# A decoder step on one core: head in a written-out order, norm sums by one ones product, padded mixing, attention projections with features on partitions

## The chip, the core and the metric

One core of a Trainium2 chip runs the whole step as one program. Its engines are TensorE (PE in the profile, PEld for its weight loads), VectorE (DVE), ScalarE (ACT), GpSimd (POOL) and SyncE (SP), which issues the transfers. The metric is the device time of one execution in microseconds; lower is better.

## The reference, cut to what matters

There are 256 prompt tokens and 64 sample tokens (320 in all, `NT`), a model width of 2048, and two layers. Everything is float32.

```python
# layer 0: gMLP over chunks of 128 tokens            # layer 1: sparse attention
z = gelu(rmsnorm(x) @ w_in);  u, v = halves(z)       p = rmsnorm(x) @ w_in;  q,k,v,iq,ik,iw = split(p)
v = rmsnorm(v)                                        q = rope(rmsnorm_per_head(q)); k = the same; iq, ik = rope
s = tril(w_s[g]) @ v_g + b_s   (per group g)          score = sum_h relu(iq_h . ik) * iw_h ; keep the top 64 (66)
x += (u * s) @ w_out                                  x += softmax(q k / sqrt(128), kept keys only) v @ w_o
# after each layer: x += (silu(conv3(g)) * conv3(up)) @ w_out,   g, up = halves(rmsnorm(x) @ w_in)
```

Outputs are x, the new keys, values and indexer keys of layer 1, the normalised v rows of layer 0 and the last rows before each convolution. `rmsnorm` divides by the root of the mean square over the features; `rope` turns each head's first half against its second half by angles that depend on the token.

## The kernel before, in words

Activations lie with features on the 128 partitions and the 320 tokens along the free axis: `xT` is 16 such tiles. Each weight block of 128x128 is the stationary operand of a matmul over 320 columns. For the precision of float32 every operand is split in two parts of the matmul's reduced type: weights in `wh` (a copy by ACT) and `wl` (the rest, by DVE), activations in `hh` and `hl` (or `rh` and `rl`). Each block then takes three matmuls, `wh·hh`, `wh·hl`, `wl·hh`, which the profile names `mm`. There are 17,328 of them. All other matmuls (`sd` in the profile: transposes, sums over partitions by a product with ones, attention scores) go to two PSUM banks of their own, `mm` results to six.

Weights arrive in units of 1 MB. A unit is split in two half-units, and 24 `mm` belong to each. `split(n + 2)` is written two half-units ahead of the matmuls that use it, and `wh` and `wl` have three buffers, so the ACT copy for half-unit n+3 can start when the matmuls of half-unit n are done. The 512 output columns of four units are one group of four PSUM banks.

Everything else is written as Python generators (`b_tile`, `norm_fin` and so on) that a small planner class (`Side`) resumes at every second block of `mm`; `yield PE` says that the next step begins with a matmul. The planner keeps an estimate of each engine's load and decides at which place in the instruction order a step is put. `S.ensure(flag)` resumes all tasks at once until the flag is there: it is called where an `mm` needs a free bank (`("ev", nbank - 6)`), or an input that a task makes (`(("o", gi), j)`: the attention of head group gi). The order that results is fixed in the program; engines run their own queues in that order.

The places that the change touches:

- The head: `x_load`, `x_tile` and the first loop passes. Tile f of x is scaled by the gain into `hh` and `hl`, squared on ACT and added into `acc` by POOL. `norm_fin(0)` then makes the factor `rs` that every result of the first stage is multiplied with when it leaves its bank.
- `norm_fin`, four times: sums over partitions by three products with a ones column, a Newton chain on 128x3 numbers, three diagonal matrices `dg`, three products with ones that spread the factors over partitions, one copy into `rs`.
- `u_tile`, 16 times: the mixing `s`. Two products of 128 rows and one of 64 rows (the sample tokens).
- Layer 1: groups in the order iq0, ik, iq1, k, v, q0, q1, q2, then the output projection o0, then q3, o1, o2, o3. For iq, k, q and v, four result tiles (heads) are collected in `tB`; `to_tok` transposes them to tokens on partitions (three bursts of four transposes), DVE applies norm and rope there, and `to_feat` transposes back (three bursts more, not for v). q and k heads also take three products with ones each for the norm.
- `attn_prompt` and `attn_sample`: four and two tasks per head group; o0 needs all six of head group 0.

Of the kernel before, what the change touches and what calls it, by code (L numbers as in the profile page):

```python
# [174 lines left out]
def trunk(ctx: ExitStack, tc: tile.TileContext, i, o):  # L175
# [60 lines left out]
    dg = com(3, 128)  # L236
# [68 lines left out]
    def norm_fin(st):  # L305
        r = tok_rstd(acc, D)
        for tt in range(3):
            w = TOKW[tt]
            dve.tensor_scalar(dg[0:w, tt, 0:w], ident[0:w, 0:w], r[0:w, tt:tt + 1], None, op0=ALU.mult)
        yield PE  # L310
        ps = sd()
        for tt in range(3):
            w = TOKW[tt]
            pe.matmul(ps[:, tt * 128:tt * 128 + w], lhsT=ones[0:w, :], rhs=dg[0:w, tt, 0:w], start=True, stop=True)
        dve.tensor_copy(rs, ps[:, 0:NT])
        S.set(("rs", st))
# [63 lines left out]
    def x_load(f, n):  # L380
        sp.dma_start(xT[:, f:f + n], i["xT"][:, f:f + n])
        for k in range(f, f + n):
            x_time[k] = S.load["dma"] + 2.2

    x_time = {}

    def x_tile(f):
        g = gT[:, f:f + 1]
        if f > 3:
            S.cur.t = x_time[f]  # L390
            yield 1
# [3 lines left out]
        yield 1  # L395
        q = yield from square_acc(("n", 0), xT[:, f], acc)
        yield 1
        add_acc(acc, q, pool)
        cnt["h", 0] = cnt.get(("h", 0), 0) + 1
        if cnt["h", 0] == NK:  # L400
            S.add(norm_fin(0), 2)

    def ws_prep():
        yield from wait(("rs", 0))
        sp.dma_start(wsT, i["a_w_sT"])
# [54 lines left out]
    def u_tile(f, ps):  # L460
# [12 lines left out]
        pe.matmul(p2[:, 256:320], lhsT=v_tok[0:64, 2, f * 128:(f + 1) * 128], rhs=wsS[0:64, f, :], start=True, stop=True)  # L473
# [161 lines left out]
    rC = cB(3, 128)  # L635
    rS = cB(3, 128)
    yn = [cB(512) for _ in range(2)]
    t2 = cB(512)
    tB = [cB(NT) for _ in range(4)]
    ssq = [cB(4, 3) for _ in range(2)]  # L640
    rq = cB(4, 3)
    rqt = cB(12)
    gq = cB(128)
# [11 lines left out]
    CM, CMS, SelH, Tm, Rep, BM = (cst[:, 0:256], cst[0:64, 256:520], cst[0:16, 520:648], cst[:, 648:712],  # L655
                                  cst[0:64, 712:968], cst[0:64, 968:1032])
    r64C, r64S = cI(3, 64), cI(3, 64)
# [3 lines left out]
    iwT = cI(64)  # L661
# [20 lines left out]
    def fold(g):  # L682
        sp.dma_start(rC, i["c_rope"][:, :, 0:128])
        sp.dma_start(rS, i["c_rope"][:, :, 128:256])
        sp.dma_start(gq, g.partition_broadcast(128))
        yield 1
        dve.tensor_tensor(rC, rC, gq[:, None, :].to_broadcast([128, 3, 128]), op=ALU.mult)
        for a, b in ((0, 64), (64, 0)):
            dve.tensor_tensor(rS[:, :, a:a + 64], rS[:, :, a:a + 64], gq[:, None, b:b + 64].to_broadcast([128, 3, 64]),
                              op=ALU.mult)  # L690

    def b_prep():
        sp.dma_start(pt_sb[0:1, :].bitcast(I32), i["page_table"])
        sp.dma_start(cst, i["c_idx"])
        sp.dma_start(r64C, i["c_rope"][:, :, 256:320])
        sp.dma_start(r64S, i["c_rope"][:, :, 320:384])
        for s in ssq:
            dve.memset(s, 1.0)
# [5 lines left out]
        yield from fold(i["b_k_norm"][0])  # L704
        S.set("gk")

    def rope(src, y, p, n, half, C, Sn):

        d = 2 * half
        sv = src.rearrange("p (h d) -> p h d", d=d)  # L710
        yv = y[0:p, 0:n * d].rearrange("p (h d) -> p h d", d=d)
        tv = t2[0:p, 0:n * d].rearrange("p (h d) -> p h d", d=d)
        dve.tensor_tensor(tv[:, :, 0:half], sv[:, :, half:d], Sn[:, None, 0:half].to_broadcast([p, n, half]), op=ALU.mult)
        dve.tensor_tensor(tv[:, :, half:d], sv[:, :, 0:half], Sn[:, None, half:d].to_broadcast([p, n, half]), op=ALU.mult)
        dve.tensor_tensor(yv, sv, C[:, None, :].to_broadcast([p, n, d]), op=ALU.mult)
        dve.tensor_tensor(yv, yv, tv, op=ALU.add)

    def to_tok(tt):
        w = TOKW[tt]
        ps = sd()  # L720
        for c in range(4):
            pe.transpose(ps[0:w, c * 128:(c + 1) * 128], tB[c][:, tt * 128:tt * 128 + w], ident)
        return ps

    def to_feat(y, tt):
        w = TOKW[tt]
        ps = sd()
        for c in range(4):
            pe.transpose(ps[:, c * 128:c * 128 + w], y[0:w, c * 128:(c + 1) * 128], ident[0:w, 0:w])
        return ps  # L730

    def b_tile(kind, gi, c, ps):
        yield from wait(("rs", 2))
        if c == 0:
            yield from take("tB")
        else:
            yield from wait(("tB", kind, gi))
        S.set(("tB", kind, gi))
        dve.tensor_tensor(tB[c], ps[:, 0:NT], rs, op=ALU.mult)
        evd(ps)  # L740
        if kind in "qk":
            yield 1
            b = yield from take("sq", 2)
            q = sqr[b]
            act.activation(q, tB[c], AF.Square)
            yield PE
            p2 = sd()
            for tt in range(3):
                w = TOKW[tt]
                pe.matmul(p2[0:w, tt:tt + 1], lhsT=q[:, tt * 128:tt * 128 + w], rhs=ones[:, 0:1], start=True, stop=True)  # L750
            s = ssq[gi % 2]
            dve.tensor_copy(s[:, c, 0:2], p2[:, 0:2])
            dve.tensor_copy(s[0:64, c, 2:3], p2[0:64, 2:3])
            give("sq", b)
        cnt["tB", kind, gi] = cnt.get(("tB", kind, gi), 0) + 1
        if cnt["tB", kind, gi] == 4:
            S.add({"iq": iq_group, "k": qk_group, "q": qk_group, "v": v_group}[kind](gi), 1)

    def iq_group(gi):
        yield from wait("bprep")  # L760
        yield from take("tok")
        for tt in range(3):
            w = TOKW[tt]
            y = yn[tt % 2]
            ps = to_tok(tt)
            if tt == 2:
                give("tB", 0)
            rope(ps[0:w, :], y, w, 8, 32, r64C[0:w, tt], r64S[0:w, tt])
            yield PE
            p2 = to_feat(y, tt)  # L770
            pv = p2.rearrange("p (c t) -> p c t", t=128)
            if tt < 2:
                copy_act(iqT(gi)[:, :, tt * 128:tt * 128 + 128], pv)
            else:
                copy_act(iqS()[:, :, 32 * gi:32 * gi + 32].rearrange("p b (c t) -> p c b t", t=8),
                         pv[:, :, 0:64].rearrange("p c (b t) -> p c b t", t=8))
            yield 1
        give("tok", 0)
# [6 lines left out]
    def v_group(gi):  # L785
        yield from take("tok")
        for tt in range(3):
            w = TOKW[tt]
            ps = to_tok(tt)
            if tt == 2:  # L790
                give("tB", 0)
            copy_act(V[0:w, tt], ps[0:w, :])
            yield 1
            sp.dma_start(o["new_v_sample"] if tt == 2 else o["new_v_prompt"][tt * 128:(tt + 1) * 128], V[0:w, tt])
        give("tok", 0)
        S.set("v")

    def qk_group(gi):
        isk = gi < 0
        yield from wait("gk" if isk else "gq")  # L800
        if gi > 1:
            yield from wait((("o", gi - 2), 0))
        yield from take("tok")
        v = ssq[gi % 2].rearrange("p a b -> p (a b)")
        dve.tensor_scalar(v, v, 1.0 / 128, EPS, op0=ALU.mult, op1=ALU.add)
        r = rq.rearrange("p a b -> p (a b)")
        rsqrt(v, r, rqt)
        yield PE
        for tt in range(3):
            w = TOKW[tt]  # L810
            y = yn[tt % 2]
            ps = to_tok(tt)
            if tt == 2:
                give("tB", 0)
            pv = ps[0:w, :].rearrange("p (h d) -> p h d", d=128)
            dve.tensor_tensor(y[0:w].rearrange("p (h d) -> p h d", d=128), pv, rq[0:w, :, tt:tt + 1].to_broadcast([w, 4, 128]),
                              op=ALU.mult)
            yield 1
            rope(y[0:w], y, w, 4, 64, rC[0:w, tt], rS[0:w, tt])
            if isk:  # L820
                sp.dma_start(o["new_k_sample"] if tt == 2 else o["new_k_prompt"][tt * 128:(tt + 1) * 128], y[0:w])
            yield PE
            p2 = to_feat(y, tt)
            pv = p2.rearrange("p (c t) -> p c t", t=128)
            if isk:
                copy_act(kT[:, :, tt * 128:tt * 128 + w], pv[:, :, 0:w])
            elif tt < 2:
# [488 lines left out]
```

## Time and profile before

| | us |
|---|---|
| median of 3 runs (lowest, highest) | 2702.72 (2702.16, 2704.13) |
| the profiled execution, its own time | 2700.93 |
| its span, first to last instruction | 2699.2 |
| PE busy | 2683.4 (99%) |
| DVE busy | 1608.0 (60%) |
| ACT busy | 1101.5 (41%) |
| POOL busy | 150.2 (6%) |

Stages in the span: gMLP layer up to about 408, its ConvFFN from 408 to 1323, attention to about 1734, its ConvFFN to the end. Nearly every instruction is issued through one helper and so carries line L149; instructions are told apart by tile names and shapes. In the chain of waits a row is a stretch of the chain of work that ended last: start, length, engine and tile, and how many instructions. A float32 product other than a transpose shows as two matmuls in the trace.

### The profile page before, as it was taken

Reading aid. Unit: us, or ns where it says so; the run is one execution under the profiler, and the core shown is the slowest. Engines: PE = TensorE matmul, PEld = TensorE weight load, DVE = VectorE, ACT = ScalarE, POOL = GpSimd, SP = SyncE. Lnnn points to the kernel's source line nnn. Section 1 sums busy time; section 2 is a strip of 40 time slices with the busy share of each in tenths; the row PEclk is TensorE's granted clock in tenths of the full one; section 3 lists DMA queues with packets and bytes.
Section 4 is the critical chain, followed back from the end, with each engine's and each line's share of the span. In section 5 each row is a group of like instructions: output and inputs, shape, how many; then the busy total and the mean of one; then the engine's idle time right before and its main releaser. Section 6 shows DMA issues by size and latency. Waiting matters only on the chain.

```text
span 2699.2 us, 44861 instructions
## 1 busy us (share of the span) xinstructions
PE 2683.4 (99%) x18425; PEld 2653.7 (98%) x18425; DVE 1608.0 (60%) x2839; ACT 1101.5 (41%) x1510; POOL 150.2 (6%) x383
## 2 busy tenths in 40 slices
PE   8999999999999999999999999999999999999999
PEld 8999999999999999999998999999999999999999
DVE  6465576646555564556558676766555645654663
ACT  5433344434433443444433344544344424433442
POOL 3000001001000010000000000001000000100100
PEclk9999999999999999999999999999999999999999
DMA  6443454444444444444543544344444444444444
GB/s 224 145 151 131 141 170 141 156 142 156 146 151 153 144 156 144 154 150 159 178 130 112 158 142 148 131 157 154 144 155 147 151 154 143 157 144 154 149 161 133
DMA packets 222479, 405.88 MB, mean 150 GB/s; under 512 B 10370, under 2 KB 35394, under 8 KB 222018
## 3 DMA queue, kind: packets, MB, share of 16 engines
q1 hardware_dynamic: 222274, 403.01, 45.3%
q8 instruction: 145, 2.38, 0.4%
q14 instruction: 60, 0.49, 0.1%
HBM read 396.82 MB, written 6.16 MB: 149 GB/s over the span
## 4 chain that ended last, share of the span: by engine, by line
PE 97%; DVE 1%; DMA 1%; issue 0%; ACT 0%; SPq 0%; DVEq 0%
PE mm L149 93%; PE sd L149 4%; DVE arena L149 1%; DVE wl L149 1%; DMA arena<-a_v_norm 0%; DMA arena<-b_q_norm 0%; ACT wh L149 0%; DMA xT<-xT 0%; SPq L149 0%; ACT scr L149 0%; DVE xT L149 0%; DVE hl L149 0%; ACT hh L149 0%; ACT arena L149 0%; ACT rh L149 0%
## 5 line engine op out<-in xcount | busy, mean ns | idle before, releaser
L149 DVE TENSOR_TENSOR wl<-raw,wh 128x1024 fp32r<-128x1024 f32 (+1 forms) x724 | 884.3, 1222 | 853.8 <-ACT wh L149 850.8
L149 ACT ACTIVATE wh<-raw 128x1024 fp32r<-128x1024 f32 (+1 forms) x724 | 765.0, 1057 | 1259.0 <-PE mm L149 1072.6
L149 PE MATMUL mm<-hh,wh 128*128 128x320 f32 x3856 | 1204.1, 312 | 5.5 <-ACT wh L149 2.9
L149 PE MATMUL mm<-hl,wh 128*128 128x320 f32 x3856 | 1192.6, 309 | 2.2 <-DVE hl L149 2.2
L149 PE MATMUL mm<-hh,wl 128*128 128x320 f32 x3856 | 1192.5, 309 | 0.2 <-DVE wl L149 0.2
L149 PEld LDWEIGHTS mm<-hh,wh 128*128 128x128 f32 x3856 | 726.7, 188 | 10.3 <-ACT wh L149 3.2
L149 PEld LDWEIGHTS mm<-hl,wh 128*128 128x128 f32 x3856 | 726.7, 188 | 2.8 <-DVE hl L149 2.7
L149 PEld LDWEIGHTS mm<-hh,wl 128*128 128x128 f32 x3856 | 726.4, 188 | 0.6 <-DVE wl L149 0.6
L149 PE MATMUL mm<-rh,wh 128*128 128x320 f32 x1920 | 597.9, 311 | 0.0
L149 PE MATMUL mm<-rl,wh 128*128 128x320 f32 x1920 | 593.2, 309 | 0.0
L149 PE MATMUL mm<-rh,wl 128*128 128x320 f32 x1920 | 593.2, 309 | 0.0
L149 PEld LDWEIGHTS mm<-rh,wh 128*128 128x128 f32 x1920 | 360.5, 188 | 0.5
L149 PEld LDWEIGHTS mm<-rl,wh 128*128 128x128 f32 x1920 | 360.5, 188 | 0.2
L149 PEld LDWEIGHTS mm<-rh,wl 128*128 128x128 f32 x1920 | 360.4, 188 | 0.0
L149 ACT ACTIVATE arena<-arena 128x336 f32<-128x336 f32 (+4 forms) x373 | 203.5, 559 | 140.6 <-DVE arena L149 131.5
L149 POOL COPY arena<-arena 128x16 f32<-128x16 f32 (+1 forms) x352 | 127.6, 401 | 1947.5 <-DVE arena L149 1529.7
L149 DVE SCALAR_TENSOR_TENSOR arena<-arena 128x336 f32<-128x336 f32 (+2 forms) x412 | 207.0, 507 | 8.7 <-ACT arena L149 0.4
L149 DVE TENSOR_TENSOR xT<-mm,xT 128x320 f32<-128x320 f32 x240 | 115.9, 487 | 82.3 <-PE mm L149 82.1
L149 DVE TENSOR_TENSOR arena<-mm,arena 128x64 f32<-128x64 f32 (+2 forms) x417 | 127.7, 344 | 51.5 <-PE mm L149 51.3
L149 DVE TENSOR_TENSOR arena<-arena 128x256 f32<-128x256 f32 (+9 forms) x372 | 135.4, 394 | 19.9 <-DMA arena<-a_v_norm 9.0
L149 PE MATMUL sd<-arena 128*128 128x128 f32 (+7 forms) x969 | 132.9, 287 | 4.6 <-ACT scr L149 2.2
L149 PEld LDWEIGHTS sd<-arena 128*128 128x128 f32 (+3 forms) x969 | 105.3, 153 | 23.6 <-issue 7.3
(36 smaller groups left out, 444.0 us busy)
## 6 DMA issues: line engine op xcount, KB each, us to landing
raw<-f_w_in SPq DMA_DIRECT2D x176, 1024.0 KB, 5.1
raw<-f_w_out SPq DMA_DIRECT2D x88, 1024.0 KB, 5.1
raw<-b_w_in SPq DMA_DIRECT2D x33, 1024.0 KB, 5.5
raw<-a_w_in SPq DMA_DIRECT2D x31, 1024.0 KB, 5.4
raw<-a_w_out SPq DMA_DIRECT2D x16, 1024.0 KB, 5.1
raw<-b_w_o SPq DMA_DIRECT2D x16, 1024.0 KB, 5.2
arena<-cache_kT SPq DMA_DIRECT2D x64, 64.0 KB, 1.9
arena<-cache_v SPq DMA_DIRECT2D x64, 64.0 KB, 3.1
```

Of the source, the lines that this page charges most:

```text
L149: return f(*a, **k)
```

## The change

1. Head: the first two cuts of weight unit 0 and the gain vector are issued from two queues; x tiles are scaled in the order that is written out (tiles 4 to 7 before the splits of half-unit 2, and so on), squares are made on ACT for four tiles at once (1280 columns) and added by DVE. Ten instead of five matmuls on ones run first.
2. `norm_fin`: one product of a ones matrix with `acc` gives the sums on all partitions, and the Newton chain runs on 128x320 numbers.
3. `u_tile`: the 64-row product becomes one of 128 rows over zeros.
4. Layer 1: norm sums, rope and scaling with features on partitions. Rope's swapped halves are made by ACT copies between partitions. k has one Newton chain for all four heads; q's factors go into the scale of the softmax. v is transposed tile by tile. k and ik go out with features on partitions (two transfers instead of six), `b_w_in` is padded by 48 columns.

```diff
 def norm_fin(st):
-    ...
+    ps = sd()
+    pe.matmul(ps[:, 0:NT], lhsT=ones, rhs=acc, start=True, stop=True)
+    dve.tensor_scalar(acc, ps[:, 0:NT], 1.0 / D, EPS, op0=ALU.mult, op1=ALU.add)
+    dve.tensor_scalar(t.bitcast(I32), acc.bitcast(I32), 1, None, op0=ALU.arith_shift_right)
+    dve.tensor_scalar(rs.bitcast(I32), t.bitcast(I32), -1.0, MAGIC, op0=ALU.mult, op1=ALU.add)
+    for _ in range(3):
+        yield 1
+        dve.tensor_tensor(t, rs, rs, op=ALU.mult)
+        dve.scalar_tensor_tensor(t, t, -0.5, acc, op0=ALU.mult, op1=ALU.mult)
+        dve.scalar_tensor_tensor(rs, t, 1.5, rs, op0=ALU.add, op1=ALU.mult)
 def x_tile(f):
-    ...
+def x_square(k):
+    act.activation(xq[k > 0], xT[:, 4 * k:4 * k + 4].rearrange("p a b -> p (a b)"), AF.Square)
+    if k:
+        dve.tensor_tensor(xq[0], xq[0], xq[1], op=ALU.add)
+    if k == 3:
+        dve.tensor_tensor(xq[0][:, 0:2 * NT], xq[0][:, 0:2 * NT], xq[0][:, 2 * NT:4 * NT], op=ALU.add)
+        dve.tensor_tensor(acc, xq[0][:, 0:NT], xq[0][:, NT:2 * NT], op=ALU.add)
+        S.add(norm_fin(0), urgent=True)
 def u_tile(f, ps):
-    pe.matmul(p2[:, 256:320], lhsT=v_tok[0:64, 2, f * 128:(f + 1) * 128], rhs=wsS[0:64, f, :], start=True, stop=True)
+    pe.matmul(p2[:, 256:320], lhsT=v_tok[:, 2, f * 128:(f + 1) * 128], rhs=wsS[:, f, :], start=True, stop=True)
+def rope(z, p, half, C, Sn, outs):
+    b = yield from take("zw", 2)
+    w = zw[b][0:p]
+    for q in range(0, p, half):
+        r = q + half if q // half % 2 == 0 else q - half
+        copy_act(w[q:q + half], z[r:r + half])
+    dve.tensor_tensor(z[0:p], z[0:p], C[0:p], op=ALU.mult)
+    yield 1
+    dve.tensor_tensor(w, w, Sn[0:p], op=ALU.mult)
+    for out, f in outs:
+        dve.tensor_tensor(out, f(z[0:p]), f(w), op=ALU.add)
+def k_stats():
+    for c in range(4):
+        pe.matmul(ps[32 * c:32 * c + 32, 0:NT], lhsT=ones[:, 0:32], rhs=sqg[:, c], start=True, stop=True)
+    ...
+    for c in range(4):
+        pe.matmul(ps[:, 0:NT], lhsT=ident[:, 32 * c:32 * c + 1].to_broadcast([128, 128]), rhs=y, start=True, stop=True)
+        dve.tensor_tensor(z, z, ps[:, 0:NT], op=ALU.mult)
+        yield from rope(z, 128, 64, CT, ST, [(z, lambda a: a)])
+def q_stats(gi):
+    for c in range(4):
+        pe.matmul(ps[32 * c:32 * c + 32, 0:SEQ], lhsT=ones[:, 0:32], rhs=sqg[:, c, 0:SEQ], start=True, stop=True)
+    copy_act(stb[:, 0:SEQ], ps[:, 0:SEQ])
+    for tt in range(2):
+        pe.transpose(ps[:, tt * 128:(tt + 1) * 128], stb[:, tt * 128:(tt + 1) * 128], ident)
+    for hf in range(2):
+        pe.matmul(ps[:, 256 + hf:257 + hf], lhsT=sqS[:, hf], rhs=ones[:, 0:1], start=True, stop=True)
+    ...
-def to_tok(tt):
-def to_feat(y, tt):
-def qk_group(gi):
-def iq_group(gi):
-    ...
 attn_prompt, attn_sample:
-    dve.tensor_scalar(n, m, -SCALE, None, op0=ALU.mult)
+    dve.scalar_tensor_tensor(n, m, -1.0, r[:, g:g + 5:4], op0=ALU.mult, op1=ALU.mult)
 the head:
+if n in (0, 2, 4):
+    for f in range(2 * n + 4, 2 * n + 8):
+        x_tile(f)
 split(n + 2)
+if n in (1, 3, 5, 7):
+    x_square(n // 2)
```

The instruction order moves at two places that matter below. First, DVE in the head, from the norm factors to the first result that leaves its bank (`arena<-mm`); the `wl` in it is that of half-unit 11, which can only be made when the matmuls of half-unit 8 are done. Before:

```order
L149 TENSOR_SCALAR arena<-arena 128x128 x2
L149 TENSOR_SCALAR arena<-arena 64x64
L149 TENSOR_TENSOR wl<-raw,wh 128x1024
L149 COPY arena<-sd 128x320
L149 TENSOR_TENSOR arena<-mm,arena 128x320 x3
```

After, where the last `wl` of the two is the same one:

```order
L149 TENSOR_TENSOR wl<-raw,wh 128x1024 x2
L149 TENSOR_SCALAR arena<-sd 128x320
L149 TENSOR_SCALAR arena<-arena 128x320 x2
L149 TENSOR_TENSOR arena<-arena 128x320
L149 SCALAR_TENSOR_TENSOR arena<-arena 128x320 x2
L149 TENSOR_TENSOR arena<-arena 128x320
L149 SCALAR_TENSOR_TENSOR arena<-arena 128x320 x2
L149 TENSOR_TENSOR arena<-arena 128x320
L149 SCALAR_TENSOR_TENSOR arena<-arena 128x320 x2
L149 TENSOR_TENSOR arena<-mm,arena 128x320 x4
```

Before, one copy stands between that `wl` and the first eviction; after, twelve operations of the norm do. On PE the eviction is waited for after half-unit 8 in both.

Second, PE at the first matmul of o0, which is the first to read `rh` of the attention (tile numbers differ between the two programs). Before:

```order
L149 MATMUL mm<-hl,wh 128x320
L149 MATMUL mm<-hh,wl 128x320
L149 MATMUL mm<-rh_14246,wh 128x320
L149 MATMUL mm<-rl_14249,wh 128x320
```

After:

```order
L149 MATMUL mm<-hl,wh 128x320
L149 MATMUL mm<-hh,wl 128x320
L149 MATMUL sd<-arena 128x128 x3
L149 MATMUL sd<-arena 32x256 x4
L149 MATMUL sd<-arena 128x64
L149 MATMUL sd<-arena 128x256
L149 MATMUL sd<-arena 128x128 x5
L149 MATMUL sd<-arena 128x256
L149 MATMUL sd<-arena 128x128 x3
L149 MATMUL sd<-arena 128x256
L149 MATMUL sd<-arena 128x128
L149 MATMUL mm<-rh_14107,wh 128x320
```

What was spread between `mm` before stands in one piece in front of o0 after: steps of head group 0's last two prompt tasks and of head group 1's first ones, which `S.ensure` wrote there.

## Rows read from the trace of the kernel before

**Rows 1.** The page, busy time of each engine:
```profile
PE 2683.4 (99%) x18425; PEld 2653.7 (98%) x18425; DVE 1608.0 (60%) x2839; ACT 1101.5 (41%) x1510; POOL 150.2 (6%) x383
```

**Rows 2.** The chain of waits over the whole span: start, us, what:
```profile
408.00 914.50 PE mm L149 x6234
```

**Rows 3.** The chain of waits, mixing of layer 0 (`u_tile`):
```profile
193.79 0.81 PE sd L149 x6
194.60 1.95 PE mm L149 x12
```

**Rows 4.** The chain of waits, four transposes of `to_tok` or `to_feat`:
```profile
1382.60 0.44 PE sd L149 x4
1383.04 4.40 PE mm L149 x30
```

**Rows 5.** The chain of waits, norm sums of one q head:
```profile
1496.84 0.54 PE sd L149 x6
1497.39 1.09 PE mm L149 x6
```

**Rows 6.** The chain of waits, 64-row transposes, a sample's scores, two transposes and a product:
```profile
1637.37 0.39 PE sd L149 x4
...
1640.61 0.94 PE sd L149 x10
...
1642.49 0.65 PE sd L149 x4
```

**Rows 7.** The chain of waits, the head:
```profile
16.50 1.61 issue
...
18.70 15.61 PE mm L149 x94
...
37.17 7.18 PE mm L149 x47
...
44.90 2.72 PE mm L149 x17
...
47.64 1.07 ACT wh L149
...
48.73 1.23 DVE wl L149
49.95 0.41 DVE arena L149
...
50.39 0.50 DVE arena L149
...
51.02 2.89 PE mm L149 x18
```

**Rows 8.** ACT in time, the first copy of weight unit 1:
```profile
14.06 1.06 ACT L149 ACTIVATE wh<-raw 128x1024 fp32r<-128x1024 f32 x1 [2.74 <-DMA raw<-a_w_in]
```

**Rows 9.** Stretches of the head: length, busy (count) by engine, granted clock, DMA:
```profile
6.50:12.20 5.70, 5.68 (x21) 5.46 (x22) 4.08 (x7) 3.65 (x8) 2.02 (x2) 1.00 0.99 368
...
16.30:22.30 6.00, 4.16 (x17) 3.79 (x16) 5.86 (x8) 4.54 (x10) 3.03 (x3) 0.72 1.04 390
```

**Rows 10.** DVE's groups by shape: busy us, mean ns, idle before:
```profile
L149 DVE TENSOR_TENSOR wl<-raw,wh 128x1024 fp32r<-128x1024 f32 x720 | 881.6, 1225 | 852.7 <-ACT wh L149 849.6 <-PE sd L149 2.2
L149 DVE SCALAR_TENSOR_TENSOR arena<-arena 128x336 f32<-128x336 f32 x352 | 197.0, 565 | 6.7 <-ACT arena L149 0.4
...
L149 DVE TENSOR_TENSOR arena<-arena 128x320 f32<-128x320 f32 x76 | 38.7, 509 | 1.8 <-ACT arena L149 1.2
...
L149 DVE TENSOR_SCALAR arena<-arena 128x320 f32<-128x320 f32 x8 | 3.1, 387 | 0.3
```

**Rows 11.** The stretch of the top-k selection (columns as in rows 9):
```profile
1440.00:1490.00 50.00, 49.54 (x344) 45.65 (x344) 46.24 (x124) 16.59 (x22) 0.15 (x1) 1.00 0.46 141
```

**Rows 12.** ACT's groups by shape (columns as in rows 10):
```profile
L149 ACT ACTIVATE arena<-arena 128x320 f32<-128x320 f32 x76 | 35.8, 474 | 37.4 <-DVE arena L149 33.5 <-PE sd L149 2.0 <-issue 1.2
...
L149 ACT ACTIVATE arena<-sd 128x384 f32<-128x384 f32 x24 | 11.4, 491 | 18.8 <-PE sd L149 18.7
```

More of the change, by code (lines that the diff above doesn't have):

```diff
@@ L305, in norm_fin @@
     def norm_fin(st):
[L306 to L309, printed above, removed]
+        b = yield from take("sq", 2)
+        t = sqr[b]
         yield PE
         ps = sd()
[L312 to L315, printed above, removed]
+        pe.matmul(ps[:, 0:NT], lhsT=ones, rhs=acc, start=True, stop=True)
[7 more added lines that the diff above has]
+            dve.scalar_tensor_tensor(rs, t, 1.5, rs, op0=ALU.add, op1=ALU.mult)
+        give("sq", b)
         S.set(("rs", st))
@@ L394, in x_tile @@
         S.set(("h", 0, f))
[L395 to L401, printed above, removed]
+    def x_square(k):
[6 more added lines that the diff above has]
+            S.add(norm_fin(0), urgent=True)
     def ws_prep():
         yield from wait(("rs", 0))
+        pool.memset(v_tok[64:128, 2, :], 0.0)
+        pool.memset(wsS[64:128], 0.0)
         sp.dma_start(wsT, i["a_w_sT"])
@@ L634, in trunk @@
     Mrep = cB(2, NT)
[L635 to L638, printed above, removed]
+    CT, ST = cB(NT), cB(NT)
+    zw = [cB(NT) for _ in range(2)]
     tB = [cB(NT) for _ in range(4)]
[L640 to L643, printed above, removed]
+    sqg = cB(4, NT)
+    sqS = cB(2, 128)
+    stb = acc
+    rqv, rqy, rqt = cB(10), cB(10), cB(10)
+    rsc = [cB(10) for _ in range(2)]
+    gcol = cB(4)
     pt_sb = cB(16)
@@ L703, in b_prep @@
         S.add(index_cache(), 1)
-        yield from fold(i["b_k_norm"][0])
+        yield from fold(0)
         S.set("gk")
[L707 to L716, printed above, removed]
@@ L718, in to_tok @@
-    def to_tok(tt):
[L719 to L723, printed above, removed]
-    def to_feat(y, tt):
[L726 to L730, printed above, removed]
+    def rope(z, p, half, C, Sn, outs):
[9 more added lines that the diff above has]
+            dve.tensor_tensor(out, f(z[0:p]), f(w), op=ALU.add)
+        give("zw", b)
@@ L732, in b_tile @@
     def b_tile(kind, gi, c, ps):
         yield from wait(("rs", 2))
[L734 to L739, printed above, removed]
-        evd(ps)
[L741 to L754, printed above, removed]
+        if kind == "k":
+            yield from k_tile(c, ps)
+            return
@@ L755, in b_tile @@
+        b = yield from take("tB", 4)
+        z = tB[b]
+        dve.tensor_tensor(z, ps[:, 0:NT], rs, op=ALU.mult)
+        evd(ps)
+        yield 1
+        yield from {"iq": iq_tile, "v": v_tile1, "q": q_tile}[kind](gi, c, z)
+        give("tB", b)
         cnt["tB", kind, gi] = cnt.get(("tB", kind, gi), 0) + 1
         if cnt["tB", kind, gi] == 4:
-            S.add({"iq": iq_group, "k": qk_group, "q": qk_group, "v": v_group}[kind](gi), 1)
-    def iq_group(gi):
+            S.add({"iq": iq_done, "v": v_done, "q": q_stats}[kind](gi), 1)
@@ L760, in iq_group, with iq_tile @@
+    def iq_tile(gi, c, z):
         yield from wait("bprep")
[L761 to L777, printed above, removed]
@@ L783, in iq_group @@
             S.add(index_done(), 1)
[L785 to L792, printed above, removed]
-            yield 1
-            sp.dma_start(o["new_v_sample"] if tt == 2 else o["new_v_prompt"][tt * 128:(tt + 1) * 128], V[0:w, tt])
-        give("tok", 0)
-        S.set("v")
-    def qk_group(gi):
-        isk = gi < 0
-        yield from wait("gk" if isk else "gq")
+        return
@@ new lines, in iq_done, with k_tile @@
+        yield
+    def k_tile(c, ps):
+        z = kT[:, c]
+        dve.tensor_tensor(z, ps[:, 0:NT], rs, op=ALU.mult)
+        evd(ps)
+        act.activation(sqg[:, c], z, AF.Square)
+        cnt["k"] = cnt.get("k", 0) + 1
+        if cnt["k"] == 4:
+            S.add(k_stats(), 1)
+        return
+        yield
+    def k_stats():
+        yield from wait("ik")
+        b = yield from take("sq", 2)
+        yield PE
+        v, y, t = sqr[b], zk, stb
+        ps = sd()
+        for c in range(4):
+            pe.matmul(ps[32 * c:32 * c + 32, 0:NT], lhsT=ones[:, 0:32], rhs=sqg[:, c], start=True, stop=True)
+        S.set("sqg")
+        dve.tensor_scalar(v, ps[:, 0:NT], 1.0 / 128, EPS, op0=ALU.mult, op1=ALU.add)
+        yield 1
+        dve.tensor_scalar(t.bitcast(I32), v.bitcast(I32), 1, None, op0=ALU.arith_shift_right)
+        dve.tensor_scalar(y.bitcast(I32), t.bitcast(I32), -1.0, MAGIC, op0=ALU.mult, op1=ALU.add)
+        for _ in range(3):
+            dve.tensor_tensor(t, y, y, op=ALU.mult)
+            dve.scalar_tensor_tensor(t, t, -0.5, v, op0=ALU.mult, op1=ALU.mult)
+            dve.scalar_tensor_tensor(y, t, 1.5, y, op0=ALU.add, op1=ALU.mult)
+            yield 1
+        give("sq", b)
+        yield from wait("gk")
+        for c in range(4):
+            yield PE
+            ps = sd()
+            pe.matmul(ps[:, 0:NT], lhsT=ident[:, 32 * c:32 * c + 1].to_broadcast([128, 128]), rhs=y, start=True, stop=True)
+            z = kT[:, c]
+            dve.tensor_tensor(z, z, ps[:, 0:NT], op=ALU.mult)
+            yield 1
+            yield from rope(z, 128, 64, CT, ST, [(z, lambda a: a)])
+        S.add(k_done(-1), 1)
@@ new lines, in k_done, with q_tile @@
+    def k_done(gi):
+        sp.dma_start(o["new_kT"], kT)
+        S.set("k")
+        yield 1
+        yield from fold(1)
+        S.set("gq")
+    def q_tile(gi, c, z):
+        if c == 0:
+            yield from wait("sqg")
+            S.flags.discard("sqg")
+            S.set(("sqg", gi))
+        else:
+            yield from wait(("sqg", gi))
+        act.activation(sqg[:, c, 0:SEQ], z[:, 0:SEQ], AF.Square)
+        act.activation(sqS.rearrange("p h (b g t) -> p g h b t", g=4, t=8)[:, c],
+                       z[:, SEQ:NT].rearrange("p (h b t) -> p h b t", b=4, t=8), AF.Square)
+        yield from wait("gq")
@@ L801, in qk_group @@
         if gi > 1:
             yield from wait((("o", gi - 2), 0))
[L803 to L807, printed above, removed]
-        yield PE
[L809 to L827, printed above, removed]
-                copy_act(qT[gi % 2][:, :, tt * 128:tt * 128 + 128], pv)
-            else:
-                for hf in range(2):
-                    copy_act(qS[gi % 2][:, hf].rearrange("p (b g t) -> p g b t", g=4, t=8),
-                             pv[:, :, hf * 32:hf * 32 + 32].rearrange("p g (b t) -> p g b t", t=8))
-            yield 1
@@ L842, in qk_group, with v_tile1, v_done @@
             S.add(attn_prompt(gi, g), 1)
+        yield 1
+    def v_tile1(gi, c, z):
+        yield PE
+        ps = sd()
+        for tt in range(3):
+            w = TOKW[tt]
+            pe.transpose(ps[0:w, tt * 128:(tt + 1) * 128], z[:, tt * 128:tt * 128 + w], ident)
+        vc = slice(128 * c, 128 * c + 128)
+        copy_act(V[:, 0:2, vc], ps[:, 0:256].rearrange("p (a b) -> p a b", b=128))
+        copy_act(V[0:64, 2, vc], ps[0:64, 256:384])
+    def v_done(gi):
+        for tt in range(3):
+            w = TOKW[tt]
+            sp.dma_start(o["new_v_sample"] if tt == 2 else o["new_v_prompt"][tt * 128:(tt + 1) * 128], V[0:w, tt])
+        S.set("v")
+        return
+        yield
     def ik_tile(c, ps):
@@ L972, in index_done @@
         yield from wait("sm")
+        yield from wait("k")
         ring_pool()
@@ L1174, in trunk @@
     ps = sd()
-    for _ in range(5):
+    for _ in range(10):
         pe.matmul(ps[:, 0:128], lhsT=ones, rhs=ones, start=True, stop=True)
-    for f in range(16):
-        S.add(x_tile(f))
     split(0)
```

158 lines of the change are left out of this document (73 added, 85 removed).

## The prediction

> **What bounds the kernel now.** I read the page first: PE is busy 99% of the span, DVE 60%, ACT 41% [rows 1], so only time that PE does not spend on `mm`, or a new wait of PE, can move the end. Then the chain of waits, for the price of one `mm`: in the first ConvFFN 6234 of them take 914.50 us, 0.1467 us each [rows 2]. All 17,328 need 2542 us. The span is 2699.2, so 157 us are something else: the other matmuls, the head, and slow or idle PE. This is all that the change can reach.
>
> The same view at the other matmuls gives their prices, as the time to the next `mm` and what the `mm` behind them take above 0.1467 each. Four transposes take 0.44 and the 30 `mm` behind them 4.40, their plain price: 0.11 per transpose [rows 4]. The sums of one q head (three products with a ones column, six passes) take 0.54, and the six `mm` behind take 1.09 in place of 0.88: 0.75 [rows 5]. Four transposes of 64 rows take 0.39, and with the same surcharge 0.60; eight passes that fill four column quarters, with two short ones, 0.94; two transposes and a product of 256 columns 0.65, which leaves 0.215 for one pass of 256 and by length 0.27 for one of 320 [rows 6]. The mixing burst takes 0.81, and the 12 `mm` behind it 1.95 in place of 1.76: 1.00 [rows 3].
>
> **Attention projections.** Removed on PE: for two iq groups, k and four q groups five bursts at 0.44 and one at 0.60, 2.8 a group, 19.6; for v three bursts, 1.3; the norm sums of 20 heads, 15.0; the indexer key's transposes, some 1.8 by the same prices. Together 37.7. Added: v four times three transposes, 1.3; the indexer key two transposes and a short product, 0.7; k's sums, eight passes of 320 columns, 1.1; k's four spreading products, two passes of 0.27 and a surcharge each, 2.8; for each q group eight passes (0.85), two transposes (0.22) and four one-column passes (0.5), 6.3. Together 12.2. That is 25.5 us less on PE, all on the path, since PE is the path. The spreading product (one column read 128 times as weights) is in no row; it lies between 0.5 like two plain passes and 1.0 like a mixing burst, and I take 0.7, near the plain passes.
>
> DVE and ACT pay for it elsewhere. By the shapes in the order, DVE's work in this stage stays about the same: the ropes change from 512 columns in tokens to 320 in features, and the small copies go. ACT gets 75 copies between partitions at about 0.47 [rows 12], 35 us beside an engine that is 41% busy; that is hidden as long as `wh` is not late, for which there are two half-units (7 us). A copy that moves data to other partitions is in no row: at worst I set it at the 1.07 of a `wh` [rows 7], 80 us, still inside ACT's idle time.
>
> **Norms and padding.** `norm_fin` has one sum burst (as in rows 5) and one of the kind in rows 3, 1.75 together; after, two passes of 0.27. Three of the four stand where nothing waits for them: 3.6 less. Their Newton chain gets longer (below, 6 us in place of about 4), but first results leave their banks after a group of 192 `mm`, 28 us, so that is covered. `u_tile`: 1.00 becomes two products, four passes of 0.11, and two passes of 64 columns at 0.06, 0.56; 16 times 0.44 is 7.0. The bounds are 0 and 7.
>
> Here a page speaks against the change. The Trainium skill, "TensorE: Matmul & The Clock Gate", Part 3, The mechanism, has it that a weight load runs beside matmuls in flight only where its row group differs from theirs. By that rule the 64-row load is the hidden one, and padding it gains nothing. The trace does not bear it out: PE's loads are busy 98% beside a PE busy 99% [rows 1], nearly all of them on full rows, and it is the bursts with 64 rows that pay the surcharge [rows 3, 6].
>
> **The head.** Before, the ninth half-unit ends at 47.62 after two stalls: at 16.5 to 18.7, and from 34.31 to 37.17, where `hh` of the last x tiles stands behind weight splits on ACT [rows 7]. Written out, `hh` of tiles 4 to 7 comes before the split of unit 1. That unit's bytes are there at 14.06 [rows 8]; `wh` 1.07 and `wl` 1.23 bring the third `mm` of unit 1 to 16.4 in place of 19.0. From there the remaining 166 `mm` to the end of half-unit 8 need 24.4: 40.8, if nothing else stalls, 6.8 earlier. It is 1.6 less where the clock falls as it did at 16.30 to 22.30 (0.72 granted) [rows 9].
>
> But then PE needs the bank of the first result, and that needs `rs`. Before, PE waited from 47.62 to 51.02: `wh` 1.07, `wl` 1.23, a copy of 0.41, an eviction of 0.50 [rows 7], since Newton on 128x3 was done before that `wl`. After, the order puts the whole chain behind it: 0.49 out of PSUM, two integer steps of 0.39, three times 0.51 and two of 0.54 (0.565 for 336 columns) [rows 10], 6.0, with hand-overs 6.3. The wait is 1.07 + 1.23 + 6.3 + 0.6, 9.2 us, and PE goes on at 50.0. So of 6.8 us 5.8 are given back. Then the clock: after the idle start PE ran at half speed (21 `mm` in 5.68 us, the 1.2 GHz level) and after the stall at 16.5 again for part of six us [rows 9], but after the 3.4 us at 47.6 it did not (18 `mm` in 2.89) [rows 7]. 9 us idle will likely bring it down; 0 to 2.8 us, I take 1.5. The head as a whole: 0.5 us slower, between 2 faster and 4 slower. Queued behind the chain on DVE are the other evictions, which PE wants only later.
>
> **New waits in the attention stage.** First, the top-k selection. From 1440 to 1490 DVE is busy 46.24 of 50 us beside a PE that is busy 49.54 [rows 11]. The change takes about 4 us of k's small matmuls out of that stretch and leaves DVE some 2 us more (one Newton chain over 320 columns, four ropes). PE gets 6 us ahead of an engine that cannot follow; the lead of `wl` covers part (7 us less 2.3 for `wh` and `wl`). I take 3, bounds 0 and 8.
>
> Second, o0. Before, head group 0's attention was ready; after, the order has its last steps in one piece in front of o0's first `mm`. When PE arrives, `wh` and `wl` for two half-units on are made first (2.3); then come a mask and maximum on 320 columns (0.5), the exponential (0.5), scaling (0.4), three transposes (0.33), their copy (0.49) [rows 4, 7, 10, 12], the product with v (0.6) and the split of its result (0.4). That is 5.5, with the queues some 7.5; PE's own part of the piece is 3.5. A net wait of 4, between 0 and 9. What is late is only o0; o1 to o3 have no such piece.
>
> **The sum.** 25.5 + 3.6 + 7.0 = 36.1 off; 0.5 + 3 + 4 = 7.5 on. The span goes from 2699.2 to 2670.6. The profiled execution took 1.7 more than its span and the median of the runs is 1.8 above that execution: 2674 us.
>
> **Rivals.**
> - No new wait shows (DVE keeps up, o0's tasks are ready, the head keeps most of its lead): 2674 less 7, less 2.5 in the head, 2664. For it: the planner kept PE without waits in the stage before. Against it: the full DVE [rows 11] and the order at o0.
> - The waits are larger: o0 9, top-k 8, the head 4, 13.5 more: 2688. For it: PE gets faster while DVE's work stays, so each chain has less cover. Against it: ACT and DVE are far from full on average [rows 1].
> - Padding gains nothing, by the rule above: the burst stays at 1.00, 2681. Rows 3 and 6 speak against it.
> - Slower than before: ACT becomes the bound of the attention stage. Place: rope's copies between partitions, on ACT ahead of `wh`. That stage has some 410 us, of which ACT, at its share of 41%, has about 240 free; 75 copies fill this at 3.2 us each, and from 3.7 each the 36 us are gone. At 4.2 us it is 75 more on PE's path: about 2740. No row is near it (0.47 for 320 columns [rows 12]), but none moves partitions.
>
> **How the numbers follow.** Forecast (2668 to 2680) 0.52; larger waits 0.18; no waits 0.14; padding in vain 0.07; ACT the bound 0.04; 0.05 for what I have not thought of, on either side of no change. The range to leave no more than two in ten outside: 2663, a little past the case without waits, to 2690, a little past the larger waits. About 0.2% (5.4 us) is what a measurement of this kernel can tell from no change: faster by more, 0.90; within, 0.04; slower by more, 0.06.
>
> **What would show it.** In the profile after: mixing bursts of 0.5 to 0.6 in the chain; no bursts of four transposes at iq and q; half-unit 8 ending near 41, then 12 DVE operations and a PE that goes on near 50; a wait of PE on ACT `rh` or DVE `rl` just ahead of the first `mm` on `rh` in the attention stage; PE waiting for DVE `wl` in the top-k stretch. ACT rows of 64x320 and 32x320 near 0.47. The prediction is wrong if bursts of full rows keep the surcharge, if copies between partitions take over 3 us, or if PE waits add up to more than 20 us in the attention stage.

## The result and the profile after

| | us | ratio to before, 95% interval |
|---|---|---|
| before, median (4 runs on the same chip) | 2702.44 | |
| after, median (4 runs, 2675.38 to 2677.56) | 2676.82 | 0.9905 [0.9892, 0.9917] |
| after, the profiled execution and its span | 2677.56, 2675.8 | |

The forecast was 2674.0, in a range from 2663 to 2690. The page of the changed kernel, busy time of each engine (to [rows 1]):

```profile
PE 2652.6 (99%) x18174; PEld 2621.7 (98%) x18174; DVE 1603.3 (60%) x2803; ACT 1130.5 (42%) x1572; POOL 135.1 (5%) x370
```

PE is as full as before with 251 fewer matmuls. Both programs issue the same 17,328 `mm`, in the same order. So the first, the 600th, the 2400th `mm` and so on of the two PE timelines are the same work, and the time between two of them (the marks, in what follows) can be compared stage by stage:

| from `mm` to `mm` | before | after | difference | forecast |
|---|---|---|---|---|
| start to the 600th (head) | 111.45 | 111.56 | +0.1 | +0.5 |
| 600 to 2400 (mixing) | 282.5 | 278.7 | -3.9 | -7.0 |
| 2400 to 2700 (second norm) | 45.8 | 45.7 | -0.1 | -1.2 |
| 2700 to 10,800 (ConvFFN, third norm, attention) | 1296.8 | 1277.3 | -19.5 | -19.7 |
| 10,800 to 11,400 (fourth norm) | 89.8 | 89.7 | -0.1 | -1.2 |
| 11,400 to the last | 869.3 | 869.3 | 0.0 | 0 |

The sum is 23.5, the difference of the spans 23.4.

The head in the chain of waits of the changed kernel (start, length, engine and tile, instructions; to [rows 7]):

```profile
15.12 24.49 PE mm L149 x165
39.63 1.06 ACT wh L149
...
40.72 1.23 DVE wl L149
41.95 0.41 DVE arena L149
...
47.84 0.50 DVE arena L149
48.34 0.14 issue
48.48 3.54 PE mm L149 x12
```

Half-unit 8 ends at 39.61 where it ended at 47.62. Then PE stands 8.87 us: `wh`, `wl`, twelve steps of the norm, the eviction. The 12 `mm` behind it take 0.295 each, twice the plain price. The stretch behind the wait (length, busy and count of PE, PEld, DVE, ACT and POOL, granted clock, DMA) shows why:

```profile
48.48:54.30 5.82, 5.82 (x23) 5.71 (x24) 3.37 (x5) 3.56 (x10) 2.01 (x1) 0.50 0.51 208
```

The granted clock is half, the 1.2 GHz level. Mixing, in the chain of waits (to [rows 3]):

```profile
193.99 0.61 PE sd L149 x6
194.60 1.82 PE mm L149 x12
```

A burst comes every 2.43 us where it came every 2.76: 0.33 less. The second norm and the start of the ConvFFN, in the same view:

```profile
398.29 0.54 PE sd L149 x2
398.83 6.03 PE mm L149 x41
...
404.88 1.07 ACT wh L149
...
405.97 1.22 DVE wl L149
...
409.39 2.74 PE mm L149 x17
```

The burst is two passes, as forecast. But PE stands from 408.21 to 409.39, and again from 1773.40 to 1774.58 at the fourth norm. The first step that reads the norm's result needs a bank back after 64 `mm`, and the Newton chain stands behind a `wl` that waited for PE at 404.86.

What PE waited for between 1380 and 1740 (us in total, times, longest), where before it waited 2.7 us:

```profile
PE sd L149 <- DVE arena L149: 3.3, 3, 2.1
PE mm L149 <- DVE wl L149: 1.3, 3, 0.5
PE sd L149 <- ACT arena L149: 1.1, 1, 1.1
PE sd L149 <- DVE rl L149: 0.7, 1, 0.7
```

Of the second row 1.0 stands in the top-k stretch, and so does 0.7 of the first row, at 1469.73; the other waits stand from 1506 on, most of them at and behind o0. PE in time at o0:

```profile
1554.10 2.45 PE L149 MATMUL sd<-arena 128*128 128x128 f32 x17
1558.65 4.23 PE L149 MATMUL sd<-arena 128*128 128x128 f32 x14 [2.10 <-DVE arena L149]
1562.54 0.60 PE L149 MATMUL mm<-rh,wh 128*128 128x320 f32 x1
```

This is the one piece that the order showed: 8.44 us from the last `mm` to the first on `rh`, for 31 passes, partly at half clock. The same 31 passes stand there in the variant early (below), where the clock stays up. The stretch in the changed kernel and in early (columns as above):

```profile
1554.10:1562.54 8.44, 6.21 (x34) 3.92 (x31) 6.00 (x26) 4.97 (x15) 0.15 (x1) 0.82 0.65 201
1544.00:1551.42 7.42, 4.98 (x34) 3.16 (x31) 5.95 (x26) 4.97 (x15) 0.15 (x1) 1.00 0.66 203
```

So 1.0 us of the piece is the clock. ACT's groups by shape (busy, mean ns, idle before) show the copies that move data to other partitions:

```profile
L149 ACT ACTIVATE arena<-arena 64x320 f32<-64x320 f32 x41 | 19.3, 470 | 13.9 <-DVE arena L149 13.0
...
L149 ACT ACTIVATE arena<-arena 32x320 f32<-32x320 f32 x34 | 15.9, 469 | 5.9 <-DVE arena L149 5.0 <-DVE scr L149 0.2
```

75 copies at 0.47 us, the price of a copy that stays on its partitions [rows 12].

### The profile page after: what moved, and what is told of

It reads as the page before. It is cut to its first block, busy times and chain, and to the rows that moved or that the text cites. A ratio compares the mean times of both kernels' runs of the same rounds, so it can differ in the third digit from the quotient of the medians.

```text
span 2675.8 us, 44338 instructions
## 1 busy us (share of the span) xinstructions
PE 2652.6 (99%) x18174; PEld 2621.7 (98%) x18174; DVE 1603.3 (60%) x2803; ACT 1130.5 (42%) x1572; POOL 135.1 (5%) x370
## 4 chain that ended last, share of the span: by engine, by line
PE 94%; DVE 3%; DMA 1%; ACT 1%; SPq 1%; issue 1%; ACTq 0%; DVEq 0%
PE mm L149 91%; PE sd L149 3%; DVE arena L149 2%; DVE wl L149 1%; SPq L149 1%; DMA arena<-a_v_norm 0%; ACT wh L149 0%; ACT arena L149 0%; DMA raw<-a_w_in 0%; DMA out_new_v_prompt<-arena 0%; DMA raw<-b_w_in 0%; DVE xT L149 0%; ACT rh L149 0%; DVE rl L149 0%; ACTq L149 0%
## 5 line engine op out<-in xcount | busy, mean ns | idle before, releaser
L149 ACT ACTIVATE arena<-arena 128x336 f32<-128x336 f32 (+6 forms) x464 | 243.8, 540 | 148.3 <-DVE arena L149 144.7
L149 DVE SCALAR_TENSOR_TENSOR arena<-arena 128x336 f32<-128x336 f32 (+5 forms) x436 | 220.4, 510 | 9.2
L149 DVE TENSOR_TENSOR arena<-arena 128x320 f32<-128x320 f32 (+6 forms) x413 | 146.4, 385 | 25.0 <-ACT arena L149 13.6
L149 PE MATMUL sd<-arena 128*128 128x128 f32 (+7 forms) x718 | 101.6, 318 | 6.6 <-DVE arena L149 3.3
L149 PEld LDWEIGHTS sd<-arena 128*128 128x128 f32 (+2 forms) x718 | 73.3, 157 | 22.0 <-issue 7.3
```

Of the source, the lines that this page charges most:

```text
L149: return f(*a, **k)
```

## Experiments

All are variants of the changed kernel but part1 and part2. Each ratio is to the kernel before, run on the same chip.

| | median us | ratio, 95% interval |
|---|---|---|
| unpad | 2680.47 | 0.9919 [0.9904, 0.9935] |
| shortnorm | 2679.06 | 0.9915 [0.9902, 0.9929] |
| early | 2667.05 | 0.9871 [0.9856, 0.9886] |
| nofold | 2670.22 | 0.9884 [0.9869, 0.9899] |
| part1 | 2698.20 | 0.9987 [0.9978, 0.9996] |
| part2 | 2684.64 | 0.9934 [0.9920, 0.9948] |
| oneshot | 2673.56 | 0.9896 [0.9881, 0.9911] |
| best | 2657.78 | 0.9837 [0.9823, 0.9850] |
| warm | 2681.45 | 0.9920 [0.9907, 0.9934] |
| warm2 | 2674.45 | 0.9892 [0.9875, 0.9908] |
| best2 | 2656.27 | 0.9829 [0.9816, 0.9842] |

**unpad: the 64-row product back.**

```diff
-pe.matmul(p2[:, 256:320], lhsT=v_tok[:, 2, f * 128:(f + 1) * 128], rhs=wsS[:, f, :], ...)
+pe.matmul(p2[:, 256:320], lhsT=v_tok[0:64, 2, f * 128:(f + 1) * 128], rhs=wsS[0:64, f, :], ...)
```

> The changed kernel with one part undone: the product for the sample tokens in u_tile takes 64 rows again instead of 128 over zeros. If padding is worth what the rows show (a mixing burst of 0.61 with 12 mm behind it of 1.82 after, 0.81 with 1.95 before: 0.33 us a burst, 16 bursts), this is 5.3 us slower than the changed kernel, about 2682, and the bursts show 0.81 and 1.95 again. If the 64-row load hides as well as a full one (the rival), the time stays at 2677 and something else made the bursts shorter.

The chain of waits has the old burst again:

```profile
195.60 0.81 PE sd L149 x6
196.41 1.95 PE mm L149 x12
```

The medians differ by 3.7 us, which their intervals alone would not separate; the stage does: 282.6 us from the 600th to the 2400th `mm`, against 278.7 padded and 282.5 before. So the padding gives 4.0 us and not the 5.3 of its bursts; where the rest went is best2's question. The rule of the Trainium skill that the prediction weighed ("TensorE: Matmul & The Clock Gate", Part 3, The mechanism), that a weight load runs beside matmuls in flight only where the row groups differ, does not tell these bursts apart in the way that the prediction read it: the bursts on full rows are the cheaper ones, 0.67 against 1.00. The same section of the Trainium skill also lets a load into a background weight buffer go ahead, which the prediction left out; no run here shows which of the two is at work.

**shortnorm: norm_fin as before, in the changed kernel.**

```diff
-    pe.matmul(ps[:, 0:NT], lhsT=ones, rhs=acc, start=True, stop=True)
-    ...  # Newton on 128x320
+    r = tok_rstd(acc, D)
+    ...  # dg, three spreading products, one copy
```

> The changed kernel with norm_fin undone: sums by a ones column, Newton on 128x3, diagonal matrices, three spreading products, all four norms. Theory: the long Newton chain behind wl in the head costs 5.5 us of PE's wait (8.87 in the changed kernel, then 3.4) and keeps the clock from falling (2.9 us: 5.8 us at half speed); the two ConvFFN starts lose their wait of 1.2 us each; each of three bursts costs 1.2 us more on PE. Net 7 us faster than the changed kernel, about 2670. Rival: PE's wait in the head is made up later, or does not come from the chain: 2677 to 2680, since the bursts cost 3.6 more.

Missed by 9 us: 2.2 us slower than the changed kernel. Its chain of waits in the head:

```profile
38.39 1.32 PE sd L149 x6
39.71 8.31 PE mm L149 x41
...
51.43 3.40 PE mm L149 x12
```

The spreading products now stand in PE's queue after the first 7 `mm` of half-unit 7, and PE waits 4.2 us for DVE there; 3.4 us at 48 stay, and the clock falls twice (12 `mm` in 3.40, 41 in 8.31). I had counted how long the chain is and not where its second PE step stands. One wait became two, and PE goes on at 51.43, later than with the long chain. So a shorter chain alone does not help; what its steps stand behind decides.

**early: the same long chain, elsewhere.**

```diff
-        if n in (1, 3, 5, 7):
-            x_square(n // 2)
+        if n in (1, 3, 4, 5):
+            x_square((1, 3, 4, 5).index(n))
+        if n == 7:                      # behind split(9), ahead of split(10)
+            for _ in norm_fin(0):
+                pass
```

> The changed kernel with the head written in another order: the squares of x tiles 8 to 15 two half-units earlier, and the whole norm (sums and Newton chain) written before the weight splits of half-units 10 and 11, so that nothing of it stands behind a split that waits for half-unit 8. Theory: PE's wait of 8.87 us at 39.6 is the order of DVE's work, and the half clock behind it (2.9 us) follows from the wait: both go, 11.8 us faster than the changed kernel, about 2665. Rivals: the lead is given back at a later wait of the gMLP layer (2670 to 2677), or PE waits for the sums of the squares instead (2672).

9.8 us faster than the changed kernel. The chain of waits:

```profile
41.02 0.50 DVE arena L149
41.52 0.14 issue
41.66 16.97 PE mm L149 x114
```

PE goes on at 41.66 in place of 48.48, after 1.2 us, and at full speed (114 `mm` in 16.97, 0.149 each). The 600th `mm` comes 9.5 us earlier, and all of that arrives at the end. Nothing is given back.

**nofold: q no longer waits for the rope tables.**

```diff
-        dve.tensor_scalar(CT, CT, gcol[:, 2 * k:2 * k + 1], None, op0=ALU.mult)   # fold, once for k, once for q
-        dve.tensor_scalar(ST, ST, gcol[:, 2 * k + 1:2 * k + 2], None, op0=ALU.mult)
 rope:
-        dve.tensor_tensor(z[0:p], z[0:p], C[0:p], op=ALU.mult)
+        dve.scalar_tensor_tensor(z[0:p], z[0:p], gcol[:, 2 * k:2 * k + 1], C, op0=ALU.mult, op1=ALU.mult)
```

> The changed kernel without folding the gains of k and q into the rope tables: the gains go in as the scalar of the rope's products (same number of DVE operations less the four that fold), the tables are loaded once, and q0's rope no longer waits for k and a second load. Theory: the one piece in front of o0 (8.4 us of sd and waits, some 4.5 net, and 1.7 us of half clock behind it) exists because q0 comes late: 5 to 7 us faster than the changed kernel, about 2671. Rival: DVE cannot follow in the top-k stretch, so q0 comes no earlier in time and PE waits elsewhere: 2675 to 2678.

6.6 us faster. PE's waits between 1380 and 1740:

```profile
PE mm L149 <- DVE wl L149: 1.2, 2, 0.7
PE sd L149 <- DVE rl L149: 0.9, 3, 0.5
PE sd L149 <- DVE arena L149: 0.7, 1, 0.7
```

The piece and its waits at o0 are gone, while the one for `wl` in the top-k stretch stays at 1.2: DVE does not take the gain back. From the 2700th to the 10,800th `mm` nofold takes 1270.4 us, 6.9 less than the changed kernel, but 5.1 less than early, oneshot and warm2 (1275.5 each). These three have the piece too, and the clock is at full speed there; so some 5 us are the edit's, and the rest is the clock, which falls at o0 in some executions only. The edit takes away q0's wait for k, the second load and the four operations that fold, all at once; which of them delays q0 most is not shown.

**oneshot: no other work between the Newton iterations.**

```diff
     for _ in range(3):
-        yield 1
         dve.tensor_tensor(t, rs, rs, op=ALU.mult)
```

> The changed kernel with the Newton chain of norm_fin written in one piece (no other work of DVE between its three iterations). Theory: PE's wait of 1.2 us at 408 and at 1773, ten us behind the norm's burst, is there because weight splits that wait for a half-unit stand between the iterations; in one piece the first results leave their banks in time: 2.4 us faster, about 2674.5, and no such wait. Rival: the chain is too long by itself (6 us beside DVE's other work) and the wait stays, or hl and wl become late: 2677.

3.3 us faster by the medians. By the marks 1.1 us comes at each of the two norms; the rest lies in the head and at o0, where the clock cost less in this execution. The chain of waits at the second norm has no break any more:

```profile
397.61 0.54 PE sd L149 x2
398.14 26.99 PE mm L149 x184
```

**part1 and part2: each half of the change alone.** part1 is the kernel before with the new head, `norm_fin` and `u_tile`; part2 has only the new attention projections.

```diff
 part1, on the kernel before:
+    norm_fin, x_tile, x_square, u_tile and the head's order of the change
 part2, on the changed kernel:
-    norm_fin, x_tile, x_square, u_tile and the head's order of the change
+    those of the kernel before
```

> The kernel before with only the first half of the change: the head in written-out order, norm_fin with one ones product and the long Newton chain, padded mixing; attention projections as before. By the marks of the two profiles the head is worth nothing (the first 600 mm end at 111.5 in both), the gMLP layer behind it 3.9 us, the norms 0.1 each where their burst stands at the start of a ConvFFN, 1.2 at the start of the attention layer: 2697, 5 us under the kernel before. Rival: the halves interact (the head's clock loss, other places of the tasks): not faster than 2702, or by more than 8.

> The kernel before with only the second half: attention projections with features on partitions; head, norm_fin and mixing as before. If the halves add, the rest of the 25.6 us is here: 20 us, 2682. The sd work removed (25.5 by the prediction's prices) less the waits for the top-k selection and for o0 (7 by the prediction) gives 2684. If the waits come from PE's lead that the head gives, and not from the projections, this is nearer 2677.

The halves give 3.7 and 17.3 us, 21.0 together, where the whole gives 25 to 26. By the marks the gMLP stage of part1 and the attention stage of part2 are as in the changed kernel (278.7 and 1277.6). What is missing is at other places. In part1 the attention layer takes 1300.5 in place of 1296.8: at its start PE waits 2.2 us for a `wl`. In the chain it stands behind a load of `b_k_norm`, for which DVE was idle 6.3 us, and of the long Newton steps only two stand between:

```profile
1323.65 3.20 DMA arena<-b_k_norm
1326.93 1.51 DVE arena L149 x4
1328.47 0.50 DVE arena L149
...
1329.40 1.23 DVE wl L149
1330.67 4.38 PE mm L149 x28
```

At 1581 the clock is at half for 6.8 us, which costs 2.9 (last section). In part2 the head, which is that of before, takes 3.1 us longer (the 600th `mm` at 114.5):

```profile
47.93 1.06 ACT wh L149
...
51.31 5.14 PE mm L149 x18
```

The wait of 3.4 us is the same as in [rows 7], but the 18 `mm` behind it take 5.14 us, not 2.89.

**warm and warm2: PE kept busy in the head's wait.** Products of ones whose results nobody reads, 66 in warm, 32 in warm2:

```diff
                     S.ensure(("ev", nbank - 6))
+                if nbank == 6:
+                    ps = sd()
+                    for _ in range(66):      # warm2: 32
+                        pe.matmul(ps[:, 0:128], lhsT=ones, rhs=ones, start=True, stop=True)
```

> The changed kernel with 66 products of ones by ones (7.3 us, results unused) put on PE in the head's wait, between half-unit 8 and half-unit 9; the wait itself stays. Theory: the granted clock falls because PE stands idle for 8.9 us, and the first 5.8 us of mm behind the wait at half speed cost 2.9 us: the clock stays at full speed and the kernel is 2.9 us faster, about 2674. Rival: the fall does not come from the idle time, or costs nothing in the end: 2677, or more where the products themselves delay half-unit 9.

```profile
40.70 15.28 PE sd L149 x134
55.98 1.77 PE mm L149 x12
```

I had priced a product as one pass: 134 passes of 0.114 (132 for the 66 products) take 15.28 us and overrun the wait by 6.4. But the 12 `mm` behind them run at full speed, and from half-unit 9 to the 600th `mm` it is 60.43 us, against 63.08 in the changed kernel: 2.65 us is what the clock costs there in that execution. In unpad, nofold, part1 and oneshot, which have the same head and the same wait, it fell too, and this stretch takes 61.7 to 62.6: the cost is 1.3 to 2.65.

> The same as 'warm' with 32 products in place of 66, since 134 passes took 15.28 us there (0.114 each, 0.228 a product): 7.3 us, which end inside the wait of 8.9 us. In 'warm' the clock stayed at full speed and the mm from half-unit 9 to the 600th took 2.65 us less than in the changed kernel. Theory: with products that fit into the wait this is the whole effect, 2.65 us faster than the changed kernel, 2674.2. Rival: the clock falls anyway when the products are fewer, or the wait grows by them: 2677 or more.

2674.45, and the 12 `mm` behind the same wait:

```profile
48.48 2.00 PE mm L149 x12
```

Useless work made the kernel about 2.4 us faster by the medians. The intervals of the two ratios overlap; the marks show it in the head, where the 600th `mm` comes 2.65 us earlier than in the changed kernel.

**best and best2: the three edits together.** best has early, nofold and oneshot, with the norm of the head in the middle of half-unit 6; best2 has one edit more.

```diff
+            if (n, m) == (6, 6):
+                for _ in norm_fin(0):
+                    pass
 best2, in v_norm:
             sp.dma_start(gbc[0:64], i["a_v_norm"][0, c].partition_broadcast(64))
-            yield 1
+            yield 12
```

> The changed kernel with all three: the norm's sums and chain in one piece in the middle of half-unit 6 and ahead of the split of half-unit 9 (squares two half-units earlier), gains as scalars in the rope, Newton chains in one piece everywhere. Adding what the single edits gave or should give (9.8 for the head and 1.2 for the wait left there at 40.5, 6.6 for q0, 2.4 for the two ConvFFN starts): 2657. Rival: they share a limit, since PE catches up with DVE in the top-k stretch or with the transfers of weights: 2661 to 2665.

> The kernel 'best' with the four products of the v rows by their gains written 12 places of the order behind their load instead of 1. Theory: DVE stands for 2.8 and 4.6 us behind a load there (a_v_norm, at 154 and 164), wl of a half-unit and the mixing's results queue behind, and PE waits 1.6 us at 166 to 168; this ate part of what the padding gave. Without it 1.2 to 1.6 us faster: 2656.4. Rival: the wl wait there has another cause, or the mixing's chain becomes later: 2658.

2657.78 and 2656.27: the single gains add. In the 140 to 200 us of best PE still waited for a `wl` that stood behind a DVE step waiting for a transfer,

```profile
PE mm L149 <- DVE wl L149: 0.7, 1, 0.7
PE mm L149 <- ACT wh L149: 0.3, 1, 0.3
```

and in best2 for nothing there. In the changed kernel PE waits 0.7 us for that `wl`, at 176.89 in its chain; the first four of the 16 mixing bursts stand ahead of it. From the 900th to the 1100th `mm`, which hold these four and the wait, it is 33.8 us in the changed kernel, 33.9 in unpad and 32.0 in best2. So the padding's missing 1.3 us are those of the first four bursts: what they gave PE, it lost again at this place, and best2 got it back. The page of best2:

```profile
PE 2645.3 (100%) x18174; PEld 2618.3 (99%) x18174; DVE 1603.0 (60%) x2799; ACT 1131.8 (43%) x1572; POOL 137.3 (5%) x370
```

## Why the prediction was right, and which terms were off

- *What bounds the kernel.* Right: every gain came out of `sd` work, waits and half-clock stretches of PE, and the time between equal `mm` did not change where neither was touched (869.3 us in both).
- *Attention projections, 25.5 off.* Right as a sum; its prices were not all tested one by one. With the third norm's 1.2 that is 26.7; nofold, where few waits are left, shows 26.4 between the 2700th and the 10,800th `mm`.
- *Top-k wait 3, o0 wait 4.* The o0 term was right: at full clock the piece takes 7.4 us, 3.9 beyond PE's own 3.5. The top-k term was too large: 1.7 us of waits there. What I had not priced is the clock at o0, 1.0 in the piece and some more behind it. That q0 comes late because it waits for k and a second load and folding of the tables was not in the prediction.
- *The head, +0.5.* Right by its steps: the half-unit ended at 39.6 (40.8 forecast), the wait was 8.9 (9.2), the clock cost 2.65 (1.5, between 0 and 2.8; 1.3 to 2.1 in the four other runs with this wait). That the sum (+0.1) came so near is luck: the half-unit came 1.2 earlier, and the clock cost 1.1 more. That the lead is given back to the order of DVE's work is shown by early, and that the clock stays up where PE is kept busy in this wait by warm and warm2. One reading was not from its row: [rows 9] give a granted clock of 1.00 from 6.50 to 12.20, and the half speed there rests on the 21 `mm` at 0.27 alone; the clock's record in that trace begins at 12.11.
- *Padding, 7.0.* Right in kind, too large. The burst fell to 0.67 and not to 0.56: two passes of 64 columns were priced by their length, but 0.67 is six times the 0.11 of a pass of 128, so a shorter pass is no cheaper here. The one-column passes of [rows 5] say nearly the same, on full rows: 0.75 for six. That makes 5.3, of which 1.3 were lost again in the waits around a load on DVE that best2 takes away.
- *Norms, 3.6.* The step "first results leave their banks after a group of 192 `mm`, 28 us, so that is covered" failed. The norm's burst stands 64 `mm` before a bank is needed, not 192, so the longer chain showed: 1.2 us lost at two places for 1.2 gained, 2.2 of the 3.6. oneshot, which takes the `wl` out from between the iterations, has no such wait.
- *Rivals.* ACT as the bound fell with the copies' 0.47 us; padding in vain fell with unpad. The larger waits did not come. The span came out 5.2 us above the forecast's 2670.6, by padding (3.1 by the marks) and norms (2.2); the median is only 2.8 above, since the profiled execution was the longest of the four.

## What to carry to other kernels

Where a split of weights waits for PE, nothing that PE itself needs next should stand behind it on the same engine: a chain of the same length, moved to another place in the queue, gave 9.8 us here, and a shorter one whose steps stood badly gave nothing. How long a chain is covered is counted to the next buffer that is needed again, not to the end of the group. An idle stretch of PE can cost twice, once as waiting and once as clock, and to compare two traces, count to the same matmul.

## What the runs showed of the hardware

The clock's fall is not settled by the length of a wait. After 8.9 us it fell in all five runs that have this wait with PE idle (the changed kernel, unpad, nofold, part1, oneshot); after the same 3.4 us it did not fall before [rows 7] and fell in part2. And there is a case with no wait at all. part1, in the chain of waits:

```profile
1581.09 1.51 PE mm L149 x6
1582.60 2.19 PE sd L149 x12
1584.79 3.50 PE mm L149 x12
```

The kernel before, the same instructions in the same order behind the same ones:

```profile
1584.80 1.07 PE mm L149 x6
1585.87 1.29 PE sd L149 x12
1587.15 1.96 PE mm L149 x12
```

The granted clock is 0.50 in the one and full in the other, and 60 `mm` later the one is 2.9 us behind. At o0 the same 31 passes ran partly at half clock in the changed kernel, unpad, part2 and warm, and at full clock in early, oneshot, shortnorm and warm2. These are single executions of programs that differ elsewhere; that one program moves by as much from one execution to the next is likely (part1's eleven lie between 2696.61 and 2701.86) but not shown by a trace. Which of two like stretches falls stays open. And copies between partitions on ACT cost no more than others, 0.47 us.
